# Spreading roots and gates over the partitions by way of memory instead of by products with the identity

## The chip, the cores and the metric

The kernel runs on one core of one Trainium2 chip. The metric is the device time of one execution in microseconds; for a program on one core that is this core's time. Engines are named as the profile names them: PE is TensorE (PEld its weight loads), DVE is VectorE, ACT is ScalarE, POOL is GpSimd, SP is SyncE, which issues nearly all loads.

## What is computed

The reference is a block of two layers over 256 latent tokens and 256 context tokens of 1024 features. Each layer has a SwiGLU feed-forward part, a mixer of four branches, and a second feed-forward part. In layer 1 the context ends at the mixer's keys and values, so that only the 256 latent tokens go on. What the change touches:

```
o = softmax(q0 k0) v - lam * softmax(q1 k1) v           (4 heads, each 128 wide)
o = o * rsqrt(mean(o*o) + EPS) * subln_g * (1 - lam_init)   (per token and head)
merged = g0*ya + g1*yb + g2*yc(o) + g3*yd
x = x + mx[5] * (merged @ w_o)                          (mixer's gate mx[5])
x = x + 0.5 * mx[8] * swiglu(norm(x))                   (second feed-forward's gate mx[8])
```

Matrix products are made of three float32r products each, of high and low halves of both sides (`mm3`, L252).

## The kernel before, in words

**Layout and staging.** Most of the work keeps features on the partitions and tokens along a row: an activation is eight tiles of 128 features by 512 tokens (X_ the latent half, C_ the context half). Weights come in tiles of 128 x 1024 (512 KB) by way of `raw_load` (L206, 6 buffers, issued by SP), are split into a high half by ACT (L218) and a low half by DVE (L222) in `split_to`, with NW = 3 buffers each for the halves, and are then used by PE in `together` (L393) with 24 products a tile of 1024 columns.

**Order of the work.** The program is traced in an order written by hand; the framework then lists instructions for each engine by their place in that order and by when its model says that they can start. Each engine, and each engine's queue of DMAs, runs its list strictly in order. Work that can wait is a generator put on a list by `later` (L408); each call of `tick` (L412) takes every such generator one step further, so that its steps lie between groups of other products.

**The attention unit** (`unit`, L793) is such a generator. One unit treats one head and one half of the tokens in two query tiles; layer 0 has 4 heads x 2 halves, layer 1 has 4 heads x 1 half, so there are 12 that reach its end. There PE sums the squares over the partitions (L842, result st), DVE makes the mean (L844, ms), POOL the root as a power (L323, ry: one column for each 128 tokens, tokens on the partitions), and a step later PE multiplies the column, repeated over 128 columns, with the identity (`bcast`, L326): the roots now lie along the row, the same on every partition, in the PSUM bank st. DVE multiplies the head's output by it (L850), ACT and DVE split the result into halves (L854, L855) in `on`, which is read by the gated sums after all heads.

**Rows in layer 1.** From the end of the mixer of layer 1 on, tokens lie on the partitions and features along the row (`rows_end`, L1055, and `ffn_rows`, L631). There a gate is needed as a row of 1024 values, the same on every partition. `spread` (L567) makes it from the gate's tile of 128 x 8 with eight products with the identity, in two PSUM tiles of the four called ax, and two copies by ACT (L574). It is called for `g1` in `rows_end` (L1096, read by `rows.add`, L597) and for `g2` after the mixer (L1305, read at the very end of the kernel). Between the two, `renorm` (L610) turns the new rows back into features on the partitions with PE transposes into ax (L621) and ACT and DVE operations on them (L627, L628, L629); its root is POOL's L323 again, and its scaling DVE's L616.

**POOL** also does the roots of the other norms, the rotary products (L709), the clearing of `pad` (L944), and few DMAs.

Of the kernel before, what the change touches and what calls it, by code (L numbers as in the profile page):

```python
# [11 lines left out]
F32 = mybir.dt.float32  # L12
# [4 lines left out]
ALU = mybir.AluOpType  # L17
PSUM = bass.MemoryType.PSUM

P = 128  # L20
D = 1024
KD = D // P
SEQ = 256
# [32 lines left out]
def f32(ap):  # L56
    return ap.bitcast(F32)
# [3 lines left out]
def backbone(ctx: ExitStack, tc: tile.TileContext, a: dict, out: bass.AP):  # L61
# [18 lines left out]
    V, S, G, PE, SP = (Engine(e) for e in (nc.vector, nc.scalar, nc.gpsimd, nc.tensor, nc.sync))  # L80
# [4 lines left out]
    tmp = ctx.enter_context(tc.tile_pool(name="tmp", bufs=1))  # L85
    sml = ctx.enter_context(tc.tile_pool(name="sml", bufs=1))
    psm = ctx.enter_context(tc.tile_pool(name="psm", bufs=NMM, space=PSUM))
    psx = ctx.enter_context(tc.tile_pool(name="psx", bufs=7 - NMM, space=PSUM))
    pst = ctx.enter_context(tc.tile_pool(name="pst", bufs=1, space=PSUM))

    n_ = [0]

    def nm(s):
        n_[0] += 1
        return f"{s}_{n_[0]}"

    def T2(dt=F32, tag="t2", bufs=NT2):
        return tmp.tile([P, T] if dt is not BF16 else [P, 2, T], dt, tag=tag, bufs=bufs, name=nm(tag))

    def A2(dt=F32R):  # L100
        return act.tile([P, T], dt, tag="a2", bufs=NA, name=nm("a2"))

    def HL(n):

        if 2 * n > T:
            return A2(), A2()
        t = A2()
        return t[:, :n], t[:, n:2 * n]

    def small(shape, dt=F32, tag="s", bufs=4):  # L110
        return sml.tile(shape, dt, tag=tag, bufs=bufs, name=nm(tag))
# [4 lines left out]
    def pax():  # L116
        return psx.tile([P, T], F32, tag="ax", name=nm("ax"))

    def pstat():
        return pst.tile([P, T], F32, tag="st", name=nm("st"))  # L120
# [131 lines left out]
    def mm3(ps, lhs, rhs, start, stop):  # L252
        (lh, ll), (rh, rl) = lhs, rhs
        PE.matmul(ps, lh, rh, start=start, stop=False)  # L254
        PE.matmul(ps, lh, rl, start=False, stop=False)  # L255
        PE.matmul(ps, ll, rh, start=False, stop=stop)  # L256
# [5 lines left out]
    def cols(t, c):  # L262
        return t[0][:, c], t[1][:, c]
# [57 lines left out]
    def rsqrt(v, n):  # L321
        y = small([P, n], tag=f"ry{n}")
        G.tensor_tensor(y, v, mhalf[:, :n], ALU.pow)  # L323
        return y

    def bcast(ps, col):  # L326
        PE.matmul(ps, col.to_broadcast([P, P]), ident, start=True, stop=True)  # L327


    sq_acc = {}  # L330

# [61 lines left out]
    def together(ws, h, cc):  # L393

        m = cc.stop - cc.start
        qs = [pmm() for _ in ws]
        for k in range(len(h)):
            for q, w in zip(qs, ws):
                mm3(q[:, :m], wk(w, k), cols(h[k], cc), k == 0, k == len(h) - 1)
        return qs  # L400
# [163 lines left out]
            evac(t, ps[t])  # L564
            tick()

    def spread(cols_):  # L567

        o = [A2(F32), A2(F32)]
        for hf in range(2):  # L570
            q = pax()
            for k in range(4):
                bcast(q[:, k * P:(k + 1) * P], cols_[:, 4 * hf + k, 0:1])
            S.copy(o[hf], q)  # L574
        return o

    class Rows:
# [102 lines left out]
    def mix(l, nrm, c, nxt, ahead=()):  # L680
        n = c.stop - c.start
# [111 lines left out]
        def unit(H, s, qt, at, es):  # L793
            qs, ks = (X_, ALL) if s == 0 else (C_, C_)
            nk = ks.stop - ks.start
            nkt = nk // P
            q0 = qs.start + qt * P
            sums = small([P, 2], tag="sums")
            nb = small([P, 2], tag="nb")
            sc = [pax() for _ in range(2)]  # L800
            for j, (x, y) in enumerate(((0, 0), (0, 1), (1, 0))):
                for m in range(2):
                    rows = slice(64 * m, 64 * m + 64)
                    PE.matmul(sc[m][:, :nk], H.q[x][rows, q0:q0 + P], H.k[y][rows, ks], start=j == 0, stop=j == 2)  # L804
            for m in range(2):
                V.tensor_reduce(nb[:, m:m + 1], sc[m][:, :nk], mybir.AxisListType.X, ALU.max)
            V.tensor_scalar(nb, nb, -0.125, None, ALU.mult)
            pr = []
            for m in range(2):
                p = T2()  # L810
                S.activation(p[:, :nk], sc[m][:, :nk], AF.Exp, bias=nb[:, m:m + 1], scale=0.125,
                             accum_out=sums[:, m:m + 1])
                pr.append(p)
            rc = small([P, 1], tag="rc")
            V.reciprocal(rc, sums[:, 1:2])
            V.tensor_scalar(rc, rc, nlam[:, l:l + 1], sums[:, 0:1], ALU.mult, ALU.mult)
            V.scalar_tensor_tensor(pr[1][:, :nk], pr[1][:, :nk], rc, pr[0][:, :nk], ALU.mult, ALU.add)
            V.tensor_scalar(es[:, qt:qt + 1], sums[:, 0:1], sums[:, 0:1], EPS, ALU.mult, ALU.mult)
            for _ in range(LAG):
                yield  # L820
            pt = pax()
            for t in range(nkt):
                PE.transpose(pt[:, t * P:(t + 1) * P], pr[1][:, t * P:(t + 1) * P], ident)  # L823
            for t2 in range(nkt // 2):
                src = pt[:, t2 * 256:t2 * 256 + 256].rearrange("p (t q) -> p t q", q=P)
                dst = [x.rearrange("p (t q) -> p t q", q=SEQ)[:, :, qt * P:(qt + 1) * P] for x in at[t2]]
                S.copy(dst[0], src)
                V.tensor_tensor(dst[1], src, f32(dst[0]), ALU.subtract)
            if qt == 0:
                return  # L830
            yield
            po = pax()[:, :SEQ]
            for t in range(nkt):
                va = cols(vv[ks.start // P + t], slice(H.hd * P, (H.hd + 1) * P))
                mm3(po, va, cols(at[t // 2], slice((t % 2) * SEQ, (t % 2 + 1) * SEQ)), t == 0, t == nkt - 1)
            sq = T2()
            S.activation(H.of[:, qs], po, AF.Identity, scale=sg[:, l:l + 1])
            S.activation(sq[:, X_], po, AF.Square)
            yield
            ps = pstat()  # L840
            for t in range(2):
                PE.matmul(ps[:, t:t + 1], sq[:, t * P:(t + 1) * P], ones, start=True, stop=True)  # L842
            v = small([P, 2], tag="ms")
            V.scalar_tensor_tensor(v, ps[:, :2], 1.0 / P, es, ALU.mult, ALU.add)  # L844
            y = rsqrt(v, 2)
            yield
            pb = pstat()
            for t in range(2):
                bcast(pb[:, t * P:(t + 1) * P], y[:, t:t + 1])
            V.tensor_tensor(H.of[:, qs], pb[:, :SEQ], H.of[:, qs], ALU.mult)  # L850
            if s == 0:
                on[H.hd] = HL(n)
            hi, lo = on[H.hd]
            S.copy(hi[:, qs], H.of[:, qs])  # L854
            V.tensor_tensor(lo[:, qs], H.of[:, qs], f32(hi[:, qs]), ALU.subtract)  # L855
# [24 lines left out]
        vn, u2, yb = [], [], []  # L880
# [155 lines left out]
        for hd in range(HEADS):  # L1036
            H = heads[hd]
            fill = qk_fill(hd + 1) if hd < HEADS - 1 else iter(())
            for s in range(ns):
                at = [(A2(), A2()) for _ in range(2 if s == 0 else 1)]  # L1040
                es = small([P, 2], tag="es", bufs=6)
                for qt in range(2):
                    later(unit(H, s, qt, at, es))
                    tick()
                    for _ in range(per):
                        if next(fill, fill) is fill:
                            next(others, None)
# [7 lines left out]
        def rows_end(rows):  # L1055
# [21 lines left out]
            for hf in range(2):  # L1077
                tot = [None, None]
                for b in range(3):
                    gt = gates(b, hf)  # L1080
                    convolve(CONV[1])
                    if hf == b == 0:
                        while len(pend):
# [10 lines left out]
            settle(done)  # L1094
            merged = {}
            g1 = spread(gate[l][1])  # L1096
            rows.h = h2 = [[tuple(act.tile([P, T], F32R, tag=f"h{x}", bufs=KD, name=nm("h" + x)) for x in "hl")
                            for _ in range(2)] for _ in range(2)]
# [101 lines left out]
        for n, (m, cc, fresh) in enumerate(order(list(range(KD)), c, back=BACK)):  # L1200
# [3 lines left out]
            if n == 0:  # L1204
                qs = dict(enumerate(together([ws[x] for x in range(JOIN)], merged, lc)))
            q = qs.pop(m) if m in qs else together([ws[m]], merged, lc)[0]
# [96 lines left out]
    rows = Rows()  # L1303
    mix(1, n4, X_, rows)
    g2 = spread(gate[1][2])  # L1305
    fg = [A2(F32), A2(F32)]
    for hf in range(2):
# [101 lines left out]
```

## Time and profile before

| what | value |
|---|---|
| median of 3 runs (lowest to highest) | 2052.14 us (2050.99 to 2052.34) |
| the profiled execution, its own time | 2052.97 us |
| its span in the trace | 2051.20 us |
| mean granted clock of PE | 0.996 of full |
| busy: PE, DVE, ACT, POOL | 99%, 71%, 36%, 3% |

The span is the time between the first and the last event of the trace; the execution's own time has 1.77 us more around it. Times in the trace are in us from the span's start. The stages that matter here: the attention units of layer 0 lie between 420 and 583 us, those of layer 1 between 1610 and 1710, the end of layer 1's mixer between 1800 and 1846, and the second feed-forward part of layer 1 after that.

### The profile page before, as it was taken

The numbers are of one execution on the slowest core, as the hardware profiler recorded it, in microseconds if no ns is written. First come the engines' busy times: TensorE is split into PE (matmuls) and PEld (weight loads), VectorE is DVE, ScalarE is ACT, GpSimd is POOL, SyncE is SP. The second block draws the span as 40 slices with busy tenths as digits, with TensorE's granted clock in tenths as the row PEclk, the third lists the DMA queues.
The fourth block names the chain that finished last, engine by engine and source line by source line (L and its number), as shares of the span: only waits on it lengthen the run. The fifth ranks groups of instructions, "written<-read, shape, count | busy, mean of one in ns | idle before, by whom it ended". The sixth has DMA issues, their size and how long they took to land.

```text
span 2051.2 us, 26809 instructions
## 1 busy us (share of the span) xinstructions
PE 2029.0 (99%) x10034; PEld 1701.4 (83%) x10034; DVE 1466.4 (71%) x2826; ACT 744.4 (36%) x1168; POOL 65.6 (3%) x92
## 2 busy tenths in 40 slices
PE   9999999999999999999999999999999999999998
PEld 6788888888888888988888898888888898877886
DVE  5997878868678446779687576964347798876665
ACT  3422223445422234422222342222234464455443
POOL 3000000001000000000000000000000010000000
PEclk9999999999999999999999999999999999999999
DMA  9575666321232323346565434653233245654563
GB/s 339 184 237 164 195 193 211 108 83 63 72 93 93 103 93 124 103 144 211 175 191 195 141 123 129 211 169 97 98 111 122 87 124 159 193 180 146 185 186 112
DMA packets 88562, 305.07 MB, mean 149 GB/s; under 512 B 10496, under 2 KB 10752, under 8 KB 88304
## 3 DMA queue, kind: packets, MB, share of 16 engines
q1 hardware_dynamic: 87984, 302.38, 46.5%
q8 instruction: 79, 1.29, 0.3%
q0 software_dynamic: 160, 0.46, 0.1%
q10 hardware_dynamic: 288, 0.52, 0.1%
q14 instruction: 51, 0.42, 0.1%
HBM read 302.27 MB, written 1.05 MB: 148 GB/s over the span
## 4 chain that ended last, share of the span: by engine, by line
PE 95%; DVE 2%; issue 1%; ACT 1%; DMA 1%; POOL 0%; POOLq 0%; ACTq 0%; DVEq 0%; SPq 0%
PE mm L254 29%; PE mm L255 28%; PE mm L256 28%; PE ax L256 2%; PE ax L255 2%; PE ax L254 2%; PE ax L77 1%; PE mm L77 1%; PE ax L804 1%; PE st L77 1%; PE ax L823 0%; POOL ry L323 0%; PE ax L327 0%; DMA raw<-in_ffn_r 0%; DVE wlo L222 0%
## 5 line engine op out<-in xcount | busy, mean ns | idle before, releaser
L218 ACT CAST whi<-raw 128x1024 fp32r<-128x1024 f32 (+1 forms) x396 | 409.2, 1036 | 986.4 <-PE mm L255 444.0
L222 DVE TENSOR_TENSOR wlo<-raw,whi 128x512 fp32r<-128x512 f32 (+1 forms) x792 | 513.4, 679 | 287.8 <-ACT whi L218 282.5
L254 PE MATMUL mm<-hh,whi 128*128 128x512 f32 (+1 forms) x1488 | 569.1, 382 | 0.6 <-DVE t L467 0.6
L255 PE MATMUL mm<-hl,whi 128*128 128x512 f32 (+1 forms) x1488 | 566.3, 381 | 0.0
L256 PE MATMUL mm<-hh,wlo 128*128 128x512 f32 (+1 forms) x1488 | 566.3, 381 | 0.0
L254 PEld LDWEIGHTS mm<-hh,whi 128*128 128x128 f32 x1488 | 279.8, 188 | 60.0 <-issue 4.7
L256 PEld LDWEIGHTS mm<-hh,wlo 128*128 128x128 f32 x1488 | 279.8, 188 | 53.8
L255 PEld LDWEIGHTS mm<-hl,whi 128*128 128x128 f32 x1488 | 279.8, 188 | 52.3
L284 DVE CUSTOM_DVE_ANT_0 t<-raw,s_b 128x1024 bf16<-128x1024 f32 x256 | 302.0, 1220 | 2.1 <-DMA raw<-in_w_ada 2.1
L255 PE MATMUL mm<-a,whi 128*128 128x512 f32 (+1 forms) x670 | 244.4, 365 | 0.0
L254 PE MATMUL mm<-a,whi 128*128 128x512 f32 (+1 forms) x670 | 244.4, 365 | 0.0
L256 PE MATMUL mm<-a,wlo 128*128 128x512 f32 (+1 forms) x670 | 244.1, 364 | 0.0
L254 PEld LDWEIGHTS mm<-a,whi 128*128 128x128 f32 x670 | 126.4, 189 | 20.2
L256 PEld LDWEIGHTS mm<-a,wlo 128*128 128x128 f32 x670 | 126.4, 189 | 20.2
L255 PEld LDWEIGHTS mm<-a,whi 128*128 128x128 f32 x670 | 126.4, 189 | 20.0
L390 DVE SCALAR_TENSOR_TENSOR X<-mm,gt,X 128x256 f32<-128x256 f32 x160 | 70.5, 479 | 87.8 <-PE mm L256 87.5
L254 PE MATMUL mm<-whi,hh 128*128 128x512 f32 (+1 forms) x336 | 128.1, 381 | 0.0
L255 PE MATMUL mm<-wlo,hh 128*128 128x512 f32 (+1 forms) x336 | 126.1, 375 | 0.0
L256 PE MATMUL mm<-whi,hl 128*128 128x512 f32 (+1 forms) x336 | 125.9, 375 | 0.0
L468 DVE TENSOR_TENSOR t<-t,mm 128x512 f32<-128x512 f32 (+1 forms) x68 | 44.4, 652 | 44.7 <-PE mm L256 44.3
L969 DVE SCALAR_TENSOR_TENSOR a<-pad,dwh,a 128x512 f32<-128x512 f32 (+1 forms) x120 | 73.9, 616 | 2.1
L254 PEld LDWEIGHTS mm<-whi,hh 128*128 128x128 f32 x336 | 63.5, 189 | 11.8 <-issue 0.7
(246 smaller groups left out, 2309.5 us busy)
## 6 DMA issues: line engine op xcount, KB each, us to landing
raw<-in_w_ada SPq DMA_DIRECT2D x128, 512.0 KB, 4.4
raw<-in_ffn_a SPq DMA_DIRECT2D x126, 512.0 KB, 4.1
raw<-in_ffn_b SPq DMA_DIRECT2D x48, 512.0 KB, 4.2
raw<-in_ffn_r SPq DMA_DIRECT2D x44, 512.0 KB, 4.5
raw<-in_w_g SPq DMA_DIRECT2D x32, 512.0 KB, 3.6
raw<-in_w_gr SPq DMA_DIRECT2D x32, 512.0 KB, 3.8
raw<-in_ffn_b SPq DMA_DIRECT2D x30, 384.0 KB, 3.4
raw<-in_ffn_s SPq DMA_DIRECT2D x22, 512.0 KB, 4.4
```

Source lines behind the costliest of these rows:

```text
L77: return tc.keep_in_program_order(f(*x, **y))
L218: S.copy(hi[:, :n], r[:, o:o + n])
L222: (eng or V).tensor_tensor(lo[:, q:e], r[:, o + q:o + e], f32(hi[:, q:e]), ALU.subtract)
L254: PE.matmul(ps, lh, rh, start=start, stop=False)
L255: PE.matmul(ps, lh, rl, start=False, stop=False)
L256: PE.matmul(ps, ll, rh, start=False, stop=stop)
L284: V.tensor_tensor_reduce(out=junk.rearrange("p a b -> p (a b)"), in0=r, in1=s_b[:, s, :], scale=1.0, scalar=0.0, op0=ALU.mult, op1=ALU.add ...
L390: V.scalar_tensor_tensor(X(m, xs), ps[:, s * SEQ - c.start:(s + 1) * SEQ - c.start], gate[l][i][:, m, s:s + 1], X(m, xs), ALU.mult, ALU.add)
L468: V.tensor_tensor(u[:, :m], u[:, :m], ps[1][:, :m], ALU.mult)
L804: PE.matmul(sc[m][:, :nk], H.q[x][rows, q0:q0 + P], H.k[y][rows, ks], start=j == 0, stop=j == 2)
L969: V.scalar_tensor_tensor(acc, src, dwh[:, ct, j:j + 1], acc, ALU.mult, ALU.add)
```

## The change

A pool of small tiles in device memory is added. `dma_spread(o, v, n)` writes the n columns of v, 128 values each, to such a tile as n rows (first transfer), and loads these rows back to all 128 partitions of o (second transfer); POOL issues both. The attention unit calls it for its two columns of roots before its `yield`, into a new tile yb_ (2 buffers) that DVE reads in place of the PSUM bank. `spread` first copies the gate's eight columns with one DVE operation and then calls `dma_spread` for each half of four columns. All other uses of `bcast` (in `rms` and `first`) stay.

```diff
+    scratch = ctx.enter_context(tc.tile_pool(name="scratch", bufs=4, space=bass.MemoryType.DRAM))
...
+    def dma_spread(o, v, n):
+
+        d = scratch.tile([n, P], F32, tag=f"d{n}", name=nm("d"))
+        G.dma_start(d.rearrange("t p -> p t"), v)
+        G.dma_start(o.rearrange("q (t p) -> q t p", p=P), d.unsqueeze(0).to_broadcast([P, n, P]))
...
-    def spread(cols_):
-
-        o = [A2(F32), A2(F32)]
+    def spread(g):
+
+        o = A2(F32), A2(F32)
+        c = small([P, KD], tag="g1")
+        V.tensor_scalar(c, g[:, :, 0], 1.0, None, ALU.mult)
         for hf in range(2):
-            q = pax()
-            for k in range(4):
-                bcast(q[:, k * P:(k + 1) * P], cols_[:, 4 * hf + k, 0:1])
-            S.copy(o[hf], q)
+            dma_spread(o[hf], c[:, 4 * hf:4 * hf + 4], 4)
         return o
...
             y = rsqrt(v, 2)
+            yb_ = tmp.tile([P, SEQ], F32, tag="yb", bufs=2, name=nm("yb"))
+            dma_spread(yb_, y, 2)
             yield
-            pb = pstat()
-            for t in range(2):
-                bcast(pb[:, t * P:(t + 1) * P], y[:, t:t + 1])
-            V.tensor_tensor(H.of[:, qs], pb[:, :SEQ], H.of[:, qs], ALU.mult)
+            V.tensor_tensor(H.of[:, qs], yb_, H.of[:, qs], ALU.mult)
```

## Rows read from the trace of the kernel before

**Rows 1.** The page, part 1: busy time of each engine, its share and instructions.

```profile
PE 2029.0 (99%) x10034; PEld 1701.4 (83%) x10034; DVE 1466.4 (71%) x2826; ACT 744.4 (36%) x1168; POOL 65.6 (3%) x92
```

**Rows 2.** The page, part 4: the chain that ended last, by engine.

```profile
PE 95%; DVE 2%; issue 1%; ACT 1%; DMA 1%; POOL 0%; POOLq 0%; ACTq 0%; DVEq 0%; SPq 0%
```

**Rows 3.** Instructions of L327: durations min/median/max in ns, first and last start.

```profile
L327 PE MATMUL st<-ident,ry x48: 270/274/275, 469.6 to 1708.7; 128*128 128x128 f32 x48
...
L327 PE MATMUL ax<-ident,gt x32: 271/275/275, 1813.3 to 1848.0; 128*128 128x128 f32 x32
```

**Rows 4.** The chain in order of time: start us, us on the chain, what.

```profile
1708.48 0.44 PE st L327 x4
...
1813.44 1.78 PE ax L327 x16
```

**Rows 5.** DVE's timeline, two of twelve units: start us, us, what.

```profile
508.84 0.15 DVE L844 SCALAR_TENSOR_TENSOR ms<-st,es 128x2 f32<-128x2 f32 x1
...
516.13 0.42 DVE L850 TENSOR_TENSOR a<-st,a 128x256 f32<-128x256 f32 x1
...
1691.42 0.15 DVE L844 SCALAR_TENSOR_TENSOR ms<-st,es 128x2 f32<-128x2 f32 x1
...
1695.79 0.42 DVE L850 TENSOR_TENSOR a<-st,a 128x256 f32<-128x256 f32 x1
```

**Rows 6.** POOL: the roots (min/median/max ns), and a DMA's issue (busy us, mean ns).

```profile
L323 POOL TENSOR_TENSOR ry<-ms,mhalf x28: 537/697/1660, 385.7 to 2045.9; 128x2 f32<-128x2 f32 x22, 128x1 f32<-128x1 f32 x4, 128x4 f32<-128x4 f32 x2
...
L77 POOL DMA_DIRECT2D t<-in_lam_p x1 | 0.6, 596 | 10.5 <-DVE a L470 10.5
```

**Rows 7.** DMA issues: queue, count, KB each, median us from issue to landing.

```profile
out_x<-a SPq DMA_DIRECT2D x2, 256.0 KB, 2.7
...
t<-in_lam_p POOLq DMA_DIRECT2D x1, 256.0 KB, 2.9
...
c_norm_g<-in_norm_g POOLq DMA_DIRECT2D x1, 48.0 KB, 6.5
cs<-in_cs SPq DMA_DIRECT2D x1, 8.0 KB, 1.7
```

**Rows 8.** Timeline of 1703 to 1709 us: splits of weight tiles.

```profile
1703.13 1.05 ACT L218 CAST whi<-raw 128x1024 fp32r<-128x1024 f32 x1 [2.03 <-issue]
...
1705.85 1.05 ACT L218 CAST whi<-raw 128x1024 fp32r<-128x1024 f32 x1 [1.67 <-PE mm L256]
...
1706.93 1.30 DVE L222 TENSOR_TENSOR wlo<-raw,whi 128x512 fp32r<-128x512 f32 x2 [1.42 <-ACT whi L218]
```

**Rows 9.** Timeline around the call for g1.

```profile
1813.86 0.42 DVE L527 TENSOR_TENSOR a<-t,a 128x256 fp32r<-128x256 f32 x1
...
1814.20 0.68 DVE L222 TENSOR_TENSOR wlo<-raw,whi 128x512 fp32r<-128x512 f32 x1
...
1814.98 0.48 PE L254 MATMUL ax<-whi,a 128*128 128x512 f32 x1
```

**Rows 10.** Timeline after the call for g2 (idle time and its end in brackets).

```profile
1849.38 0.55 POOL L323 TENSOR_TENSOR ry<-ms,mhalf 128x1 f32<-128x1 f32 x1 [4.62 <-DVE ms L607]
...
1851.14 0.48 DVE L616 TENSOR_SCALAR a<-X,ry 128x512 f32<-128x512 f32 x1
...
1851.93 1.97 PE L621 MATMUL ax<-ident,a 128*128 128x128 f32 x8 [3.65 <-ACT a L574]
...
1853.44 0.61 ACT L218 CAST a<-raw 128x512 fp32r<-128x512 f32 x1
...
1854.10 1.22 PE L254 MATMUL mm<-a,hh 128*128 128x512 f32 x2 [0.20 <-ACT a L218]
...
1856.39 0.63 PE L256 MATMUL mm<-a,hl 128*128 128x512 f32 x1
...
1856.82 0.63 PE L254 MATMUL mm<-a,hh 128*128 128x512 f32 x1
```

**Rows 11.** Windows: PE, PEld, DVE, ACT, POOL busy us (count), PE clock, DMA.

```profile
1840.00:1860.00 20.00, 15.85 (x72) 12.91 (x71) 16.87 (x34) 12.19 (x26) 1.10 (x2) 0.83 0.45 145
```

## Prediction

> **What bounds the kernel now.** I read the busy shares first, then the chain that ended last, then the timelines of the places that the change touches. PE is busy for 99% of the span [rows 1] and makes 95% of the chain [rows 2]: what PE no longer does is gained, if its next operands are there, and what another engine does counts only where PE comes to wait for it. POOL is nearly idle, so the question is not how much work it gets but how long its answer takes and who stands behind it.
>
> **What is removed.** The trace has 48 records of the roots' products and 32 of the gates' [rows 3]. A column takes two records, so these are 24 columns (12 units of two) and 16 columns (two calls of eight). A record lasts 0.27 us, but they overlap: on the chain a unit's four records take 0.44 us, and one call's sixteen take 1.78 us [rows 4]. The price is the second figure, not 80 times the first.
>
> *Units.* PE runs on without a pause before and behind these products, and no later product of PE needs the root soon: `on` is read after all heads. So the whole 12 x 0.44 = 5.3 us is gained, as long as the new wait (below) stays covered.
>
> *g1.* PE's next products after the call begin at 1814.98 [rows 9]. Without the 1.78 us they could begin at 1813.2, but the third of them reads the low half that L527 ends at 1814.28, and the fifth the low half of the weights that L222 ends at 1814.88 [rows 9]. A product of 512 columns takes 0.227 us (12 of them in the 2.72 us between two splits of a tile, 1703.13 to 1705.85 [rows 8]). Four products before 1814.88 is 1813.97, so 1.0 us is gained here, and DVE is late next. Bounds: 0, if DVE's later sums on the same path eat it, and 1.8.
>
> *g2.* PE's transposes wait 3.65 us, until 1851.93, for ACT's copy of the spread tile [rows 10]. That looks like 3.65 us to gain, but the second scaling by L616 ends only at 1851.62 [rows 10]: with the same order the transposes gain 0.3 us. The first product behind them waits for ACT's split at 1853.44 [rows 10], before which ACT loses two copies of 512 columns; a cast of that size takes 0.61 us there, so at most 1.2 us. I take 0.7, between the two. The upper end is a rival (below).
>
> **What is added.** Each unit gets two POOL transfers, each call of `spread` four: 12 x 2 + 2 x 4 = 32 issues, at 0.6 us each [rows 6] about 19 us of POOL's time, spread over a POOL that is 97% idle. The two DVE copies of 128 x 8 cost about as much as a small L844, 0.15 us [rows 5], and fall beside other work.
>
> The path that counts runs from L844 to L850. Before, it took 7.3 us in a middle one of the twelve units and 4.4 us in the shortest, the third of layer 1 [rows 5]: there the products stood in PE's list well behind the root. After, it is L844 (0.15), the root (0.70 at the median, 0.54 to 1.66 [rows 6]), and two landings in a row, since the second transfer must wait for the first. No row shows a transfer of single values to memory. Bounds of one landing: 1.7 us (8 KB) and 6.5 us (the POOL load at the start, beside all the others); a POOL load of 256 KB in a quieter stretch took 2.9 us, a store of 256 KB 2.7 us [rows 7]. I take 2.9 for each, the nearest row by queue and size. Sum: 0.15 + 0.70 + 5.8 = 6.7 us, bounds 4.1 and 14.8. So in most units yb_ is there when DVE comes to it, and in the shortest one DVE, which runs in order, waits 2.3 us.
>
> The Trainium skill (DMA: Bandwidth & Descriptors, section Rules for kernel authors) says that a strided last dimension is lowered to one descriptor for each element. By that the first transfer has 256 pieces where the 256 KB load has at least 128 rows; no row here prices such a piece, and with a first landing at the upper bound the sum of the path would be 10.3 us.
>
> What waits behind DVE then? The splits of weights, and PE behind them. A tile in layer 1 lasts 2.72 us; three buffers let the split run two tiles ahead, 5.4 us, less the split itself (1.05 by ACT, 1.30 by DVE [rows 8]): a cover of 3.1 us. In layer 0 a tile feeds 24 products of 512 columns, 5.4 us, and the cover is 8.5 us. So 2.3 us cost nothing; without that cover they would cost 2.3 us. POOL's queue holds the second transfer until the first has landed; behind it stand rotary products and other roots, which here come several us apart, and the framework lists them by when they can start. g1 and g2 are read some 20 us after the call and at the end, so their landings are hidden.
>
> **Sum.** 5.3 + 1.0 + 0.7 = 7.0 us off the profiled execution's 2052.97 gives 2046.0; the median of the runs is 0.8 below that execution, so I predict 2045 for the median.
>
> **Rivals.**
>
> *Slower: DVE held by a late yb_.* If a landing takes far more than 2.9 us, L850 holds DVE, the splits behind it come late, and PE idles in layer 1's units. For it: DVE is the second busiest engine [rows 1], and POOL's root took up to 1.66 us instead of 0.70 [rows 6], so something slows POOL at times. The Trainium skill (SBUF — State Buffer, section Who interferes with whom) says that POOL's work, the writing of its transfers' descriptors included, can be blocked by DVE operations that use a port which both share; the spread of the root's durations agrees, and nothing here shows it for a transfer. Price: against the middle unit's 7.3 us, the cover of 3.1 is used up at a path of 10.4 us, landings of 4.8 each. Landings of 6 give a path near 13.2, 2.8 us beyond the cover in four units, 11 us, and 2056 in all. At the upper bound of 14.8 it is 4.4 x 4 = 17.6 us, and after each such pause PE runs at 1.2 GHz for a while: behind the 3.65 us pause products come 0.43 us apart instead of 0.227 from 1854.10 to at least 1856.82 [rows 10], in a window with a mean clock of 0.83 [rows 11]; that is half of 2.7 us, 1.3 each, 5 us in all, and 2068. It outweighs the gain from landings of about 5.6 us on. Against it: only the load at the start took so long. Chance 0.15.
>
> *No change: POOL's root of the last norm stands behind g2's transfers.* The root at 1849.38 [rows 10] lies on the chain into the second feed-forward part. If g2's two pairs come in POOL's queue just before it, each second transfer holds the queue for a landing, 2 x 2.9 = 5.8 us: 2051. Against it: the gate is long known, so the first transfers can go early. I count here also other orders that give the gain back. Chance 0.17.
>
> *Faster still.* Freed of two ax tiles and two copies, the stretch from 1846 to 1857 is listed anew, and the pause of 3.65 us and the slow products behind it (1.3) go as well: 5.0 instead of 0.7, 2041. Against it: L616 at 1851.14 [rows 10] depends on none of what is removed. Chance 0.13.
>
> **How the numbers follow.** The forecast, 2045 with 2041 to 2048.5 by its own bounds, has 0.55. About 0.2% (4.1 us) is what a measurement of this kernel can tell from no change. Faster by more: nearly all of the forecast (0.52) and the faster rival (0.13), 0.65. Slower by more: 0.16, the slower rival and a little of the others. The rest, 0.19, is no change. The range from 2039 to 2053 takes in the faster rival and the unchanged case and leaves out most of the slower one and little below.
>
> **What would show it.** Right: no L327 records on st and none from gt; PE's records fewer by 80; POOL with 32 transfers; a landing near 3 us; L850 without long waits for a DMA; PE without pauses between 420 and 583 and between 1610 and 1710; the window after the call for g2 at a similar clock. Wrong: L850 among the long waits of DVE, ACT's or DVE's splits late and PE waiting for them, a clock under 1.00 in the units; or L323 of the last norm waiting on a transfer, with PE's pause before the transposes longer than 3.65 us; or a landing above 5 us.

## The result, and the profile after

The changed kernel takes 2136.08 us (median; 2134.56 to 2138.45) against 2052.01 for the kernel before on the same chip: a ratio of 1.0409, interval 1.0396 to 1.0421, 84 us slower. I had forecast 2045 and a range up to 2053. Sign and size are both wrong.

I read the profile of after in the order of the prediction. The busy shares come first, the page's part 1; it answers to [rows 1]:

```profile
PE 2054.0 (96%) x9954; PEld 1714.3 (80%) x9954; DVE 1463.0 (68%) x2828; ACT 741.7 (35%) x1164; POOL 89.8 (4%) x124
```

PE has its 80 records fewer (10034 to 9954), POOL its 32 transfers more (92 to 124). The edit is in. But the span is 2136.7 instead of 2051.2, 85.5 more, and it splits in two: PE is idle 82.7 us instead of 22.2 (span less busy time), 60.5 more; and it is busy 25.0 us longer, with less to do, which is the mark of a slower clock (0.974 granted on average, 0.996 before). The page's part 2, in 40 slices of 53 us, shows where:

```profile
PE   8999999997789999999999999999999978998998
...
PEclk9999999997789999999999999999999988999999
```

The dips of PE and of the clock lie in slices 10 to 12 and 33 to 34: layer 0's units and layer 1's. The windows over those stretches give columns of us, busy us (instructions) of PE, PEld, DVE, ACT and POOL, granted clock, DMA share, GB/s:

```profile
460.00:660.00 200.00, 165.22 (x729) 131.65 (x728) 104.09 (x252) 62.00 (x140) 24.51 (x31) 0.85 0.34 60
1700.00:1800.00 100.00, 77.93 (x491) 70.52 (x490) 56.84 (x137) 38.91 (x82) 12.85 (x17) 0.86 0.38 89
```

In the kernel before, the first of these stretches reads so (same columns):

```profile
460.00:660.00 200.00, 200.00 (x997) 165.79 (x996) 155.17 (x321) 77.16 (x158) 12.93 (x16) 1.00 0.26 81
```

DVE does a third less in the same 200 us, so it is held, not loaded. By what, the waits of after tell (engine, buffer and line that waits, whom for: us in total, times, the longest):

```profile
DVE a L856 <- DMA yb<-d: 116.3, 12, 11.9
...
ACT a L860 <- DVE a L856: 80.1, 9, 11.5
POOL yb L335 <- DMA d<-ry: 80.1, 10, 9.3
...
PE st L849 <- ACT t L845: 42.4, 8, 8.5
...
PE mm L258 <- DVE wlo L224: 5.9, 1, 5.9
```

L856 is DVE's product with `yb_` (L850 before), L335 the second transfer of `dma_spread`. All twelve units wait, 9.7 us each on average. The landing times stand among the DMA issues (queue, count, KB, median us to landing):

```profile
yb<-d POOLq DMA_DIRECT2D x12, 128.0 KB, 4.2
...
t<-in_lam_p POOLq DMA_DIRECT2D x1, 256.0 KB, 3.0
d<-ry POOLq DMA_DIRECT2D x12, 1.0 KB, 8.7
...
d<-g POOLq DMA_DIRECT2D x4, 2.0 KB, 9.1
```

One kilobyte to memory takes 8.7 us, three times as long as the 256 KB load above it. Now one unit from end to end, the first of layer 0, in the timeline of after (start us, us, engine, line, operation; in brackets the idle time before and what ended it):

```profile
465.41 0.15 DVE L851 SCALAR_TENSOR_TENSOR ms<-st,es 128x2 f32<-128x2 f32 x1
...
465.64 1.67 POOL L325 TENSOR_TENSOR ry<-ms,mhalf 128x2 f32<-128x2 f32 x2 [20.09 <-DVE ms L880]
...
467.27 0.79 POOL L334 DMA_DIRECT2D d<-ry  x1
...
472.03 0.68 DVE L224 TENSOR_TENSOR wlo<-raw,whi 128x512 fp32r<-128x512 f32 x1
...
476.74 0.59 POOL L335 DMA_DIRECT2D yb<-d  x1 [7.18 <-DMA d<-ry]
...
479.55 0.39 PE L258 MATMUL mm<-hh,wlo 128*128 128x512 f32 x1
481.44 0.42 DVE L856 TENSOR_TENSOR a<-yb,a 128x256 f32<-128x256 f32 x1 [8.73 <-DMA yb<-d]
...
483.24 0.75 DVE L824 SCALAR_TENSOR_TENSOR t<-t,rc,t 128x512 f32<-128x512 f32 x1
...
484.08 0.38 ACT L845 ACTIVATE t<-ax 128x256 f32<-128x256 f32 x1 [8.62 <-DVE t L824]
...
484.51 1.01 PE L849 MATMUL st<-ones,t 128*128 128x1 f32 x4 [4.58 <-ACT t L845]
```

From L851 to L856 it is 16.0 us. DVE stood at L856 from 472.71 on, 7.3 us after L851. Behind it in the list stands a *later* unit's softmax: L824 waits only for DVE, which has just been released, ACT's squares (L845) for the next unit's sums wait for L824, and the sums of PE (L849) need the squares. PE has products to run until 479.9 and then nothing. So the wait of 8.73 us cost a pause of 4.58, and the clock after it.

The product has not kept its place in DVE's list. In the kernel before, the same unit reads:

```profile
463.17 0.15 DVE L844 SCALAR_TENSOR_TENSOR ms<-st,es 128x2 f32<-128x2 f32 x1
...
471.98 0.75 DVE L817 SCALAR_TENSOR_TENSOR t<-t,rc,t 128x512 f32<-128x512 f32 x1
472.64 0.42 DVE L850 TENSOR_TENSOR a<-st,a 128x256 f32<-128x256 f32 x1
```

There the softmax (L817, now L824) stood *ahead* of the product. The other units agree: eight of the twelve are followed by another softmax of their layer, and in all eight that stood ahead of the product before and stands behind it after. In ten of the twelve, fewer of DVE's operations now lie between L851 and the product than lay between L844 and the product. Before, DVE was ready for the product 2.4 to 10.6 us after L844 (7.3 on average); after, it is ready 2.0 to 7.7 us after L851 (5.3 on average). So two things came together: the roots take longer to arrive, and the framework, with PE's product gone, lists the reader sooner.

Three marks before, after and between tell what each stretch lost. They are rows of a line's instructions (min/median/max ns, first and last start us), first of the kernel before:

```profile
L356 DVE TENSOR_SCALAR ms<-st x8: 159/160/163, 385.4 to 1585.7; 128x2 f32<-128x2 f32 x8
...
L874 DVE TENSOR_SCALAR ms<-mv x4: 160/165/170, 463.2 to 1800.1; 128x4 f32<-128x4 f32 x2, 128x2 f32<-128x2 f32 x2
...
L607 DVE TENSOR_SCALAR ms<-ss,ss x4: 214/214/215, 1843.9 to 2045.6; 128x1 f32<-128x1 f32 x4
```

and the same three of after:

```profile
L364 DVE TENSOR_SCALAR ms<-st x8: 159/160/163, 387.7 to 1641.2; 128x2 f32<-128x2 f32 x8
...
L880 DVE TENSOR_SCALAR ms<-mv x4: 159/167/170, 465.5 to 1885.8; 128x4 f32<-128x4 f32 x2, 128x2 f32<-128x2 f32 x2
...
L614 DVE TENSOR_SCALAR ms<-ss,ss x4: 213/214/216, 1928.7 to 2131.1; 128x1 f32<-128x1 f32 x4
```

The first mark is 2.3 late (ahead of every unit, so not the change), the last one of layer 1's first norm 55.5: layer 0's eight units lost 53.2. The next is 85.7 late: layer 1's four units lost 30.2. The first L614, behind g1, is 84.8 late and the last 85.5: g1's stretch gained 0.9 and g2's lost 0.7, together next to nothing. Per unit that is 6.7 us in layer 0 and 7.5 in layer 1.

### The profile page after: what moved, and what is told of

Its sections match the earlier page's. It is cut to its first block, busy times and chain, and to the rows that moved or that the text cites. A ratio compares the mean times of both kernels' runs of the same rounds, so it can differ in the third digit from the quotient of the medians.

```text
span 2136.7 us, 26687 instructions
## 1 busy us (share of the span) xinstructions
PE 2054.0 (96%) x9954; PEld 1714.3 (80%) x9954; DVE 1463.0 (68%) x2828; ACT 741.7 (35%) x1164; POOL 89.8 (4%) x124
## 3 DMA queue, kind: packets, MB, share of 16 engines
q0 software_dynamic: 1568, 3.10, 0.8%
## 5 line engine op out<-in xcount | busy, mean ns | idle before, releaser
L256 PE MATMUL mm<-hh,whi 128*128 128x512 f32 (+1 forms) x1488 | 575.9, 387 | 0.4 <-DVE t L475 0.4
L257 PE MATMUL mm<-hl,whi 128*128 128x512 f32 (+1 forms) x1488 | 572.1, 384 | 0.0
L256 PEld LDWEIGHTS mm<-hh,whi 128*128 128x128 f32 x1488 | 284.4, 191 | 61.3 <-issue 6.0
L258 PEld LDWEIGHTS mm<-hh,wlo 128*128 128x128 f32 x1488 | 284.2, 191 | 60.9 <-DVE wlo L224 6.2
L257 PEld LDWEIGHTS mm<-hl,whi 128*128 128x128 f32 x1488 | 284.6, 191 | 53.5
L856 DVE TENSOR_TENSOR a<-yb,a 128x256 f32<-128x256 f32 x12 | 5.1, 425 | 116.3 <-DMA yb<-d 116.3
```

The source lines that it names most:

```text
L856: V.tensor_tensor(H.of[:, qs], yb_, H.of[:, qs], ALU.mult)
```

## The experiments

The theory: the whole loss is the wait at L856, because the first transfer lands late and DVE's list has a later unit's chain behind it. The rivals: the gates, the traffic of the transfers, POOL's way of issuing them, ACT's part of the chain. Diffs are against the kernel after. Each ratio is against the kernel before as it ran beside that kernel on the same chip, so losses are compared, not bare times.

**Each half alone.** The first kernel puts the units' products back, the second the gates'.

```diff
-            yb_ = tmp.tile([P, SEQ], F32, tag="yb", bufs=2, name=nm("yb"))
-            dma_spread(yb_, y, 2)
             yield
-            V.tensor_tensor(H.of[:, qs], yb_, H.of[:, qs], ALU.mult)
+            pb = pstat()
+            for t in range(2):
+                bcast(pb[:, t * P:(t + 1) * P], y[:, t:t + 1])
+            V.tensor_tensor(H.of[:, qs], pb[:, :SEQ], H.of[:, qs], ALU.mult)
```

> The gates go by way of memory, the attention's roots by products as before. If the 12 waits of L856 (116 us in the trace of after) are the whole loss, this run is where the gates' part of the forecast put it: 0 to 2 us under before, 2050 to 2052. If the long landing of the gates' transfers or their place in POOL's queue is a part of the loss, it is above before, by up to 10 us.

Measured: 2051.80 against 2053.09, ratio 0.9996 (0.9987 to 1.0005), no difference that can be told. The transfers of the gates land late too, but nobody waits for them. The pause ahead of the transposes stayed; the timeline of this kernel has them, with the first product behind them:

```profile
1849.71 2.12 PE L628 MATMUL ax<-ident,a 128*128 128x128 f32 x8 [4.15 <-DVE a L623]
1852.89 1.22 PE L256 MATMUL mm<-a,hh 128*128 128x512 f32 x2 [1.05 <-ACT a L220]
```

It now ends with DVE's second scaling instead of ACT's copy (3.65 us [rows 10]), as the prediction had it, but it is half a microsecond longer, and the first product waits 1.05 us behind it instead of 0.20.

```diff
-    def spread(g):
-
-        o = A2(F32), A2(F32)
-        c = small([P, KD], tag="g1")
-        V.tensor_scalar(c, g[:, :, 0], 1.0, None, ALU.mult)
+    def spread(cols_):
+
+        o = [A2(F32), A2(F32)]
         for hf in range(2):
-            dma_spread(o[hf], c[:, 4 * hf:4 * hf + 4], 4)
+            q = pax()
+            for k in range(4):
+                bcast(q[:, k * P:(k + 1) * P], cols_[:, 4 * hf + k, 0:1])
+            S.copy(o[hf], q)
```

> The attention's roots go by way of memory, the gates by products as before. If the units' waits are the whole loss: 2135 to 2139, the time of after or the gates' 1 to 2 us above it. If the gates share in the loss: below 2130.

Measured: 2139.31, ratio 1.0419 (1.0405 to 1.0433), as slow as the whole change. The units are all of the loss.

**Transfers without a reader.** All transfers are issued as in the change, and DVE multiplies by PE's products as before.

```diff
             dma_spread(yb_, y, 2)
             yield
-            V.tensor_tensor(H.of[:, qs], yb_, H.of[:, qs], ALU.mult)
+            pb = pstat()
+            for t in range(2):
+                bcast(pb[:, t * P:(t + 1) * P], y[:, t:t + 1])
+            V.tensor_tensor(H.of[:, qs], pb[:, :SEQ], H.of[:, qs], ALU.mult)
```

> The units issue both transfers as in after, but DVE reads the roots from the products as before and nobody reads yb_; the gates go by memory. Theory (the wait of DVE on the landing): within 5 us of before, 2048 to 2057. Rival (the transfers themselves: POOL's queue held for some 10 us a unit, many pieces of 4 bytes beside the weights' loads): 2090 or more, since they are all still there.

Measured: 2056.57, ratio 1.0018 (1.0009 to 1.0027). The first landing is as long as ever (9.0 us), and the loss is 3.5 us instead of 84: what costs is the waiting, not the traffic or the issuing. DVE's list has the softmax ahead of the product here, as in the kernel before. The 3.5 that stay come up again below.

**The product later in DVE's list.** The product comes two `yield`s later, and the edge `behind(V)` puts it behind DVE's last instruction so far that is no split of weights. With that the softmax stands ahead of it again, as before the change.

```diff
             dma_spread(yb_, y, 2)
-            yield
-            V.tensor_tensor(H.of[:, qs], yb_, H.of[:, qs], ALU.mult)
+            for _ in range(3):
+                yield
+            with behind(V):
+                V.tensor_tensor(H.of[:, qs], yb_, H.of[:, qs], ALU.mult)
```

> As after, but L856 is put two steps of the generators later in DVE's list, behind what DVE has been given by then (some 14 us more than the 7 it had). Theory (the wait): the path of about 13 us is covered, L856 waits little, and the gain of 5 us by fewer products shows: 2043 to 2050. Rival (products and waits aside, the transfers disturb): stays above 2090. If only part of the wait goes, the chain from L856 over ACT to the next unit's squares is the one to look at.

Measured: 2055.99, ratio 1.0014 (1.0005 to 1.0023); 81 of the 84 us are gone. DVE's wait for the transfer:

```profile
DVE a L865 <- DMA yb<-d: 10.0, 3, 7.2
```

But it was not faster than before. One pause of PE is left in layer 0, and the timeline of this kernel shows its cause on POOL:

```profile
506.97 0.59 POOL L342 DMA_DIRECT2D yb<-d  x1 [8.55 <-DMA d<-ry]
507.58 0.74 POOL L723 TENSOR_TENSOR t<-t,c_rope 128x256 f32<-128x256 f32 x1
508.35 0.42 DVE L724 TENSOR_TENSOR t<-t,t 128x256 f32<-128x256 f32 x1 [3.09 <-POOL t L723]
...
511.37 0.70 PE L818 MATMUL ax<-a,a 64*128 64x256 f32 x6 [1.76 <-ACT t L825]
```

The second transfer holds POOL's queue for 8.55 us until the first has landed, and a rotary product behind it, which has nothing to do with the roots, comes late; DVE waits 3.09 us for it and PE 1.76 us further on. The kernel with unread transfers has a pause in the same 6 us (PE 4.51 of 6 busy, the clock 0.93 there and 0.78 in the next 6).

**Both held back.** The second transfer, too, is issued two steps later, behind POOL's last instruction so far.

```diff
         G.dma_start(d.rearrange("t p -> p t"), v)
+        yield
+        yield
+        with behind(G):
+            dma_rows(o, d, n)
...
-            dma_spread(yb_, y, 2)
-            yield
-            V.tensor_tensor(H.of[:, qs], yb_, H.of[:, qs], ALU.mult)
+            yield from dma_spread(yb_, y, 2)
+            for _ in range(2):
+                yield
+            with behind(V):
+                V.tensor_tensor(H.of[:, qs], yb_, H.of[:, qs], ALU.mult)
```

> As the run with L856 put later, but the second transfer of a unit also stands two steps later in POOL's list, behind the rotary product that POOL then has. Theory (POOL's queue, held 8 to 9 us by the second transfer before a rotary product, made the one pause of PE that was left in that run, 1.8 us and a slow stretch behind it): PE has no pause in layer 0's units, and the gain of the products left out shows, 2045 to 2050. Rival (the transfers cost their 4 us by other means, as contention of the loads): 2054 to 2058 again.

Measured: 2054.34, ratio 1.0010 (1.0001 to 1.0019): not the theory's time, but one in the rival's range. Layer 0 is as the theory had it, without a pause (PE is busy 139.3 of the 140 us from 460 to 600). One long wait is left, at layer 1's end, where the steps between are short, and PE has a pause of 2.4 us beside it; DVE's timeline of this kernel:

```profile
1703.95 0.43 DVE L872 TENSOR_TENSOR a<-yb,a 128x256 f32<-128x256 f32 x1 [6.94 <-DMA yb<-d]
```

The last kernel below takes this wait away and so decides between the two.

**What makes the landing long.** Three kernels change the first transfer alone. In the first each partition's two values go to neighbouring places, so 128 pieces of 8 bytes are written instead of 256 of 4.

```diff
-        G.dma_start(d.rearrange("t p -> p t"), v)
+        G.dma_start(d.rearrange("t p -> (t p)").rearrange("(p t) -> p t", t=n), v)
```

> As after, but the first transfer writes each partition's values one behind the other (128 pieces of 8 or 16 bytes instead of 256 or 512 of 4), so it leaves out the turning of columns into rows and the roots land in the wrong order. If the number of pieces sets the landing of 8.7 us: about 5 us, and some 40 us less in all, near 2095. If a store of small pieces costs this whatever their number (the way through memory, the queue): landing 8 us or more, and above 2125.

Measured: 2075.72, ratio 1.0113 (1.0098 to 1.0129). Landing and loss are both below what the first case expected. The landing is 3.3 us instead of 8.7, and DVE's wait:

```profile
d<-ry POOLq DMA_DIRECT2D x12, 1.0 KB, 3.3
```

```profile
DVE a L856 <- DMA yb<-d: 53.9, 12, 7.7
```

That is 62.4 us less of waiting for 61.0 us less of loss (84.1 to 23.1): between these two kernels a microsecond of this wait costs a microsecond.

The second has ACT's queue issue the transfer.

```diff
-        G.dma_start(d.rearrange("t p -> p t"), v)
+        S.dma_start(d.rearrange("t p -> p t"), v)
```

> As after, but ACT's queue issues the first transfer instead of POOL's, with the same pieces. If the writing of its descriptors on POOL is what makes it slow: landing 3 to 4 us, and 50 to 60 us less in all, 2075 to 2090. If the small pieces in memory do: landing 8 us or more, and 2125 or more.

Measured: 2138.57, ratio 1.0415 (1.0400 to 1.0429), and the landing is the same:

```profile
d<-ry ACTq DMA_DIRECT2D x12, 1.0 KB, 8.7
```

So neither POOL's queue nor its writing of descriptors makes it long. The page's part 3 also counts the pieces here; one queue's packets and MB, of the kernel before and of this one:

```profile
q10 hardware_dynamic: 288, 0.52, 0.1%
q10 hardware_dynamic: 5664, 0.55, 0.2%
```

The 5376 packets more are 12 x 256 + 4 x 512, one for each value, and 16 more for each of the 16 transfers. In after, the same transfers show 32 packets each on POOL's queue (1568 there, 1056 here), and land no sooner. The third repeats each value 16 times, so that as many pieces (256 for a unit) are written, of 64 bytes each.

```diff
-        d = scratch.tile([n, P], F32, tag=f"d{n}", name=nm("d"))
-        G.dma_start(d.rearrange("t p -> p t"), v)
+        d = scratch.tile([n, P, 16], F32, tag=f"d{n}", name=nm("d"))
+        w = small([P, n, 16], tag=f"w{n}", bufs=1)
+        V.tensor_scalar(w, v.unsqueeze(2).to_broadcast([P, n, 16]), 1.0, None, ALU.mult)
+        G.dma_start(d.rearrange("t p x -> p t x"), w)
...
```

> As after, but DVE first repeats each value 16 times and the first transfer writes pieces of 64 bytes, as many as in after (256 or 512), each to a place of its own; the second transfer then reads the first of them, so the values it spreads are not the roots. If the number of pieces costs the time: landing 8 us or more, and above 2125. If it is that they are 4 bytes and side by side in memory: landing 3.5 to 5 us, and 2075 to 2095.

Measured: 2073.22, ratio 1.0093 (1.0078 to 1.0108); the transfers of the units and of the gates:

```profile
d<-w POOLq DMA_DIRECT2D x12, 16.0 KB, 2.0
...
d<-w POOLq DMA_DIRECT2D x4, 32.0 KB, 3.3
```

As many pieces, 16 times the bytes, and a landing of 2.0 us instead of 8.7: the number of pieces is not the cost either. What is left is that pieces of 4 bytes lie side by side in memory. Whether it is their size or that they are neighbours is not told apart. Landing and time are a little below the second case's ranges. DVE's waits of this kernel:

```profile
DVE a L859 <- DMA yb<-d: 38.2, 12, 6.4
...
DVE w L335 <- POOL ry L325: 9.3, 11, 1.3
...
DVE w L335 <- DMA d<-w: 2.7, 2, 1.5
```

DVE waits 15.7 us less for `yb_` than with the 8-byte pieces, yet the loss is only 2.3 us less. The other two rows show why: the repeat (L335) stands in DVE's list and waits there for POOL's root, and twice for a buffer, 12.0 us together. All three make 50.2 us against 53.9.

**ACT's place in the chain.** ACT's copy behind the product, which it waited 80.1 us for, is moved two steps later.

```diff
-            S.copy(hi[:, qs], H.of[:, qs])
+            yield
+            yield
+            with behind(S):
+                S.copy(hi[:, qs], H.of[:, qs])
```

> As after with its wait of L856, but ACT's copy behind it (L860, and the low half) comes two steps later in ACT's list. If the pauses of PE come by way of ACT (L860 waits for L856 and stands before the next unit's squares, which PE's L849 waits for): most of the 42 us of these waits go, 2085 to 2100. If DVE's own list is enough (L856 stands before operations that PE waits for): within 15 us of after, 2121 to 2140.

Measured: 2140.76, ratio 1.0426 (1.0411 to 1.0440), nothing gained, as the second case had it to within a microsecond. The first of PE's waits in this kernel:

```profile
PE st L856 <- ACT t L852: 14.7, 3, 6.5
PE ax L837 <- DVE t L831: 9.8, 2, 6.9
PE mm L265 <- DVE wlo L230: 7.8, 3, 6.2
```

PE now comes to wait for DVE's softmax and DVE's splits as well. That ACT's list was needed for the loss falls; DVE's own is enough, and what it holds back varies.

**A version without the waits.** As "both held back", but in layer 1 each gap is three steps, and the units that are still open are finished two passes later.

```diff
...
+            yield from dma_spread(yb_, y, 2, 2 + l)
+            for _ in range(2 + l):
+                yield
+            with behind(V):
+                V.tensor_tensor(H.of[:, qs], yb_, H.of[:, qs], ALU.mult)
...
-        later(spatial())
+        sp = later(spatial())
...
                     if hf == b == 0:
+                        settle(sp)
+                    if hf == 0 and b == 2:
                         while len(pend):
```

> As the spaced run, with one step more ahead of each of the two in layer 1, whose steps are shorter, and with the last units of layer 1 left to run out over two more sweeps of gates instead of being finished at once before them. There the spaced run had its last long wait of L872, 6.9 us, and a pause of PE of about 3 us with a slow stretch. Theory: that pause goes too, no wait of DVE for yb is left, and the time is 2045 to 2049, below before by the products left out. Rival (the transfers cost some us by their presence): 2051 or more with no such wait left.

Measured: 2049.62 against 2052.44, ratio 0.9985 (0.9976 to 0.9994): the best of the kernels, 2.8 us (0.14%) under before. The interval leaves out 1, but the gain is below the 0.2% that I had set as the bound. The time lies between the theory's 2049 and the rival's 2051; with two short waits left (below), the transfers' presence costs nothing that outweighs the gain, and the rival falls. Its busy shares, one wait and two of the three marks:

```profile
PE 2022.4 (99%) x9954; PEld 1693.1 (83%) x9954; DVE 1464.9 (72%) x2828; ACT 743.1 (36%) x1164; POOL 86.7 (4%) x124
```

```profile
DVE a L872 <- DMA yb<-d: 5.4, 2, 2.8
```

```profile
L377 DVE TENSOR_SCALAR ms<-st x8: 158/159/160, 385.1 to 1583.3; 128x2 f32<-128x2 f32 x8
...
L896 DVE TENSOR_SCALAR ms<-mv x4: 159/164/174, 462.9 to 1796.4; 128x4 f32<-128x4 f32 x2, 128x2 f32<-128x2 f32 x2
```

PE is busy 6.6 us less than before. The marks are 0.3, 2.4 and 3.7 us early: about 2.1 us are gained by layer 0's units and 1.3 by layer 1's stretch. This kernel also changes the order of work at layer 1's end, and no run has that order with PE's products, so how much of the 1.3 us comes from the products is not shown. The landings are no shorter (9.3 and 6.1 us); DVE now comes to the product late enough for nearly all of them.

## Why the prediction was wrong

*What PE no longer does.* Here the direction was right and the size too large. The units' products were put at 5.3 us; with the long waits gone, at most 3.4 us of them show in the trace (2.1 and 1.3), and 2.8 us in the times, which hold the gates too. The step "gained, as long as the new wait stays covered" had the right condition. Even with a free path, the whole gain stays below the 0.2% that can be told from no change.

*g1 and g2.* Forecast 1.7 us together; the time of the gates alone (0.9987 to 1.0005) holds that and nothing alike. The marks say more. In after g1's stretch gained 0.9 us, near the 1.0 of the sum, but g2's lost 0.7 where the sum had a gain of 0.7. That their landings are hidden, and that g2's pause stays because the second scaling is late next, held; that the pause and the wait behind it grow was not foreseen.

*The landing, the first step that failed.* "I take 2.9 for each, the nearest row by queue and size." The second landing was 4.2, the first 8.7, above my upper bound of 6.5. The row that I leaned on, a load of 256 KB, is near by queue alone: it has neither 4-byte pieces nor memory as its target. The path was forecast at 6.7 us with bounds of 4.1 to 14.8; the first unit took 16.0. I had written that no row shows a transfer of single values to memory, and then took an upper bound from a row of another kind as if it closed the question. The Trainium skill (DMA: Bandwidth & Descriptors, section Rules for kernel authors) points the right way with its descriptor for each element of a strided last dimension, and by it I had reckoned 10.3 us for the path; the runs agree on the count (the packets on ACT's queue) and on the direction, but not on a cost by the count, as 256 pieces of 64 bytes landed in 2.0 us.

*The cover, the second step that failed.* "What waits behind DVE then? The splits of weights." I reckoned how far the splits run ahead, 3.1 us in layer 1 and 8.5 us in layer 0, and so held layer 0 to be safe. What stands behind the product in the kernel after is first of all a later unit's softmax, and PE's next sums come late by it. In the first unit 4.15 us of the 8.73 were covered (8.73 less the pause of 4.58), in layer 0, where I had 8.5; the slower clock after the pause takes back part of that. Over the twelve units a wait of 9.7 us became a pause of 4.7 (34.8 and 22.1 us of idle PE in the two windows, over 12) and 2.1 us more of busy time (25.0 over 12). Only one long pause was one for a split, 5.9 us in layer 1's first unit: there DVE had waited 7.85 us, so the splits covered 1.9 of it where I had 3.1.

*The gap as slack, the third step that failed.* I compared the new path with the 7.3 and 4.4 us that the old gap had, as if DVE's list would stay as it was. It did not: the product moved up in it, ahead of the softmax, and DVE was ready for it 5.3 us after L851 on average, where it had been 7.3. The old list behind L850 would not have shown this; the list of the changed kernel does. That the framework reckons with shorter transfers is the likely reason, argued and not shown. "The product later" undoes the move and gives DVE more time at once, and no run does the first alone, so how much of the loss is the move and how much the long landing is not told apart. With the move and landings of 3.3 and 4.2 us the loss was still 23.1 us.

*The rivals.* The slower one had the mechanism, DVE held by a late `yb_`, and the point from which it decides (landings of about 5.6 us; the mean of the two was 6.45). It had the price wrong: 2056 to 2068, since it counted only layer 1's four units and only the splits. All twelve units paid, about 7 us each. Its sum slips too: landings of 6 make a path of 12.9, not 13.2, so 10 us and not 11, and it sets a gap of layer 0, 7.3 us, against the cover of layer 1. Its reason, POOL's port (the Trainium skill, SBUF — State Buffer, section Who interferes with whom), is not what the runs show: POOL issued the first transfer in 0.74 to 0.79 us, and from ACT's queue the landing is the same. POOL's queue behind a second transfer, which I had waved aside, made a pause of 1.76 us in "the product later". Taking it away cleared layer 0, but the intervals of the two kernels (1.0005 to 1.0023 and 1.0001 to 1.0019) do not tell a gain. The rival of no change did not come about: POOL issued the gates' first transfers at 1198.5 and 1432.3 us, long before the last norm, and its root did not stand behind the second ones. The pause that the faster rival hoped to lose stayed.

## What to carry to other kernels

A wait on an in-order engine is priced by everything that stands behind it in that engine's list, above all by the next rounds of the same loop, and not by the work that first comes to mind. That list can change with the edit: where a reader loses a step that it had to wait for, look up its new place before taking the old gap as slack. An operation that no row shows has no upper bound from rows of other kinds: where the forecast hangs on it, the range must hold the time that a several times longer one gives, in every place where it is used. Going by way of memory in place of a short product on the critical engine gained here only with the reader and the second transfer both moved behind other work by hand, and then less than 3 us of 2052.

## What was not expected of the hardware

A store of 256 single values of 4 bytes side by side in memory (1 KB) landed in 8.7 us, of 512 (2 KB) in 9.1; 128 pieces of 8 bytes took 3.3, 256 pieces of 64 bytes 2.0, and a load that spreads the 1 KB over 128 KB on chip 4.2. Twice the pieces cost no more than the kernels differ among themselves (medians of 8.7 to 9.3 for 256 pieces, 8.5 to 9.7 for 512), and the queue (POOL's or ACT's) made no difference.

A POOL queue that waits for a landing delays POOL's unrelated work: 8.55 us of waiting became 3.09 us on DVE and 1.76 us on PE.

The pauses cost more than their own length. In layer 0's stretch the granted clock fell to a mean of 0.85, between the levels of 2.4 and 1.2 GHz, where it had been 1.00; PE was busy 25.0 us longer over the whole kernel with 80 records fewer.
